# Attention scores of a head pair: products on 64 array rows per head instead of stacked high and low parts

## The chip, the cores and the metric

The kernel runs on one core of one Trainium2 chip. The metric is the device time of one execution in microseconds, the median of several runs. In the profile the engines are PE (TensorE, the matrix products; PEld its weight loads), DVE (VectorE), ACT (ScalarE), POOL (GpSimd) and SP (the queue that issues all DMAs here).

## The reference

One inference step of a two-layer decoder for a prompt of 512 tokens and 8 samples of one token each, width 1024, all in float32. Layer 0 has a gated convolution (A) and a dilated sliding-window attention (B), layer 1 a pooling mixer (C) and a retention (D). The change touches the prompt part of mixer B alone: 16 heads of 64 features; three patterns of window and dilation with ALiBi, each with its own softmax, and the three merged by their denominators.

```
for w, d in DIL_PATTERNS:            # (128,1), (512,4), (2048,16)
    ...
    s = jnp.einsum('bnirhd,bnjrhd->bnrhij', qs, kk)
    ...
    s = jnp.where(valid[None, :, None, None], s + bias, -jnp.inf)
    m = jnp.max(s, axis=-1, keepdims=True)
    p = jnp.exp(s - m)
    l = jnp.sum(p, axis=-1)
    o = jnp.einsum('bnrhij,bnjrhd->bnirhd', p, vv) / ...
...
return combine_patterns(outs, lses)
```

Merged by denominators, the three softmaxes are one softmax over all causal positions with the bias -slope x distance + log(number of patterns that hold the position); that bias is a constant array of the kernel.

## The kernel before

**Products in parts.** Each float32 operand is cut in a high part, which TensorE multiplies exactly (type fp32r), and a low part, the remainder. A large product is the sum of high x high, high x low and low x high.

**Tiles.** The input projection is worked off in tiles of 128 output features and all 520 tokens (512 of the prompt, 8 samples). A tile has 8 steps over the 1024 input features; a step (`mm3`) has six products into a tile `mm`: three parts, each in a half of 256 and a half of 264 columns. `advance` prepares the weights of later tiles at set steps: ACT writes the high half (whi), DVE the low half in two pieces (wlo).

**Order.** The order of every engine is the order in which the Python code calls it. Between two steps `tick` takes pieces of smaller work from four lists: `at(n, ...)` runs a piece n ticks later without fail, `put(..., after=n)` queues it so that one is taken per tick, ordered by its due tick, `put_fill` takes one when no `put` is due, and `put2` one every second tick. Each engine works through its own instructions strictly in that order and waits where an operand or a buffer is not ready. Small results go into a ring of four PSUM tiles `aux`, each 128 x 512.

**A head pair.** `head_pair(p)` works on two heads, 128 features, in four tiles: v, k, gate, q, so 32 ticks. What follows from the q tile of a pair therefore runs between the steps of the next pair's tiles. The pieces, with e for the head (0 or 1) and qb for a block of 128 queries:

- `k_dup`, right after the k tile: four DMAs that write each head's 64 rows of k (tile kf) to both halves of a tile kd of 128 rows. `k_split(e)`, 7 and 9 ticks after the k tile: ACT writes the high part of kd, two ticks later DVE the low part.
- After the q tile ACT writes the high part of q to the rows of the head and, a tick later, `q_lo` (DVE) the low part to the other 64 rows, scaled by -1/8. So a product of 128 rows adds high and low part of q in one go.
- `score(e, qb)`: two products, with the high and with the low part of kd, into one aux tile, over the first N = max(256, 128 (qb + 1)) keys. Then a row on DVE (L521) adds the bias and takes the minimum (the sign is turned), the next tick ACT takes the exponent with its sum ls, and two ticks later `norm` divides by the sum, on ACT for odd qb and on DVE for even.
- `turn(e, g)`: up to four transpositions of 128 x 128 of the weights into an aux tile, grouped by block of keys; `turn(e, 0)` takes the first 128 keys of all four query blocks. ACT writes the high part of it at once, DVE the low part a tick later.
- `weigh(e, jb)`: the products with v into an aux tile that stays open over jb 0 to 3.
- Beside these: `v_out` (four transpositions of v, ACT copies them and writes their high part, DVE the low part two ticks on), `q_rows` and the window scores of the samples (`window_scores`, `window_sums`, DVE), and products of the adaLN weights (`ada_mm`, on 32 columns).

The ticks after the end of the q tile at which they come due are Q0 = 5 plus a number from a table: `score(0, .)` 0, 1, 3, 4; `score(1, .)` 6, 7, 9, 10; `turn(0, .)` 11, 13, 15; `turn(1, .)` 17, 20, 22; `weigh(0, .)` 18, 19, 21, 23; `weigh(1, .)` 25 to 28.

Of the kernel before, what the change touches and what calls it, by code (L numbers as in the profile page):

```python
# [14 lines left out]
ALU = mybir.AluOpType  # L15
# [3 lines left out]
P = 128  # L19
# [10 lines left out]

# columns of the packed constants
C_ID = 0
# [54 lines left out]
def hybrid_kernel(ctx: ExitStack, tc: tile.TileContext, a, o):  # L87
# [91 lines left out]

# [1 line left out]
    now, seqn = [0], [0]  # L181
# [34 lines left out]

# [1 line left out]
    csm = cp.tile([P, C_W], F32, name="csm")  # L218
# [21 lines left out]

# [1 line left out]
    w_in = [a["w_in_e"], a["w_in_o"]]  # L242
# [61 lines left out]
    def advance(k):  # L304
        # weights of the tiles that come next, a part at each step of this tile
        if k == 1 or (k == 5 and n_split[0] < cur[0] + 2):
            w_hi()
        if k in (3, 6):
            w_lo((0,))
        if k in (4, 7):  # L310
            w_lo((1,))
        if k in (5, 7) and n_raw[0] < n_split[0] + 4:
            w_raw()
# [15 lines left out]

# [1 line left out]
    def ada_load(layer, kind, j):  # L331
# [35 lines left out]

# [1 line left out]
    def h_hi(layer, j, xp, xs):  # L369
# [12 lines left out]

# [1 line left out]
    warm = cp.tile([P, 1], F32, name="warm")  # L384
# [62 lines left out]
    load(csm[:, P:C_W], a["c_small"][:, P:C_W])  # L447
# [1 line left out]
    yB, yA = [None] * KT, [None] * KT  # L449
# [7 lines left out]
    def head_pair(p):  # L457
# [14 lines left out]

        def k_dup(kf):
            st["kd"] = []
            for e in range(2):
                kd = tt(S)
                for h in range(2):
                    load(kd[64 * h:64 * h + 64], kf[64 * e:64 * e + 64])
                st["kd"].append(kd)

        def k_split(e):
            kh, kl = tr(S), tr(S)
            act(kh, st["kd"][e])
            at(2, lo_of, kl, st["kd"][e], kh)
            st["k", e] = (kh, kl)

# [20 lines left out]

        def score(e, qb):
            if qb == 0:
                st["bt"] = bt[e]  # L510
                st["mn", e], st["ls", e] = mk(cp, [P, 4], F32, "mn", 4), mk(cp, [P, 4], F32, "ls", 4)
                st["E", e] = []
            n, N = (qb + 1) * P, max(H0, (qb + 1) * P)
            kh, kl = st["k", e]
            mn, ls = st["mn", e][:, qb:qb + 1], st["ls", e][:, qb:qb + 1]
            s = aux([P, S])
            qs = st["q", e][:, qb * P:(qb + 1) * P]
            mm(s[:, 0:N], qs, kh[:, 0:N], True, False)
            mm(s[:, 0:N], qs, kl[:, 0:N], False, True)
            sb = tt(n)  # L520
            nc.vector.tensor_tensor_reduce(  # L521
                out=sb, in0=s[:, 0:n], in1=bt[e][:, S - n:S], scale=1.0, scalar=3e38, op0=ALU.add, op1=ALU.min,
                accum_out=mn,
            )
            st["E", e].append(sb)
            at(1, act, sb, sb, ACTF.Exp, mn, -1.0, ls)
            at(3, norm, e, qb)
# [49 lines left out]

        # v, k, q and gate tiles, each followed by what depends on it
        vps = ps01[0] if p == 0 else z_tile(0, 48 + p, h0)
# [7 lines left out]
        sample_z(0, 40 + p, kps)  # L587
        at(0, k_dup, kf)
        at(1, load, o["k_t"][p], kf)
        at(7, k_split, 0)  # L590
        at(9, k_split, 1)
        gps = z_tile(0, 56 + p, h0)
# [7 lines left out]
        qps = z_tile(0, 32 + p, h0)  # L600
        for e in range(2):
            r = slice(64 * e, 64 * e + 64)
            st["q", e] = tr(S)
            act(p2(st["q", e][r]), qps[r, :, 0:H0], ACTF.Copy, scale=-0.125)

        def q_lo():
            for e in range(2):
                r, r_ = slice(64 * e, 64 * e + 64), slice(64 - 64 * e, 128 - 64 * e)
                stt(p2(st["q", e][r_]), qps[r, :, 0:H0], -0.125, p2(f(st["q", e][r])), ALU.mult, ALU.subtract)
            sample_z(0, 32 + p, qps)  # L610

        at(1, q_lo)
        for e, fn, ticks in (
            (0, score, (0, 1, 3, 4)), (1, score, (6, 7, 9, 10)), (0, turn, (11, 13, 15)), (0, weigh, (18, 19, 21, 23)),
            (1, turn, (17, 20, 22)), (1, weigh, (25, 26, 27, 28)),
        ):
            for i, n in enumerate(ticks):
                put(fn, e, i, after=Q0 + n)
# [8 lines left out]

# [1 line left out]
    uc = mk(cp, [P, KT, 15 + NB], F32, "uc", 1)[:, :, 0:2 + 2 * NB]  # L629
# [9 lines left out]
    def soft_scores():  # L639
        # softmax over window rows and the new row, (batch, head) on partitions  # L640
        prod = tt(P).rearrange("p (b k e) -> p b k e", b=NB, k=KT)
        nc.gpsimd.memset(prod, 0.0)
        for e in range(2):
            r = slice(64 * e, 64 * e + 64)
            vtt(prod[r, :, :, e].rearrange("p b k -> p k b"), zs[0][r, 32:40, :], zs[0][r, 40:48, :], ALU.mult)
        st = aux([P, 257])
        for t in range(2):
            nc.tensor.transpose(st[:, t * P:(t + 1) * P], scores[:, t].rearrange("p b h -> p (b h)"), ident)
        mm(st[:, 256:257], prod.rearrange("p b k e -> p (b k e)"), on_d[:, 0:1], True, True)
        bd = csm[:, C_BD:C_BD + 257]  # L650
        sc = tt(257)
        stt(sc[:, 0:256], st[:, 0:256], 0.125, bd[:, 0:256], ALU.mult, ALU.add)
        stt(sc[:, 256:257], st[:, 256:257], 128.0, bd[:, 256:257], ALU.mult, ALU.add)
        sm = mk(cp, [P, 2], F32, "sm", 1)
        nc.vector.tensor_reduce(out=sm[:, 0:1], in_=sc, op=ALU.max, axis=AX.X, negate=True)
        act(sc, sc, ACTF.Exp, bias=sm[:, 0:1], accum_out=sm[:, 1:2])
        nc.vector.reciprocal(sm[:, 1:2], sm[:, 1:2])
        vts(sc, sc, sm[:, 1:2], None, ALU.mult)
        soft["sc"] = sc
        put(soft_turn, after=4)  # L660
# [27 lines left out]
    def window_weigh(b0):  # L688
        # two batches at a time: rows (batch, half of the heads, head), columns (head in the half, feature)
        pd = aux([P, 512])  # L690
# [106 lines left out]

# [1 line left out]
    def out_tile(layer, m, ps, halves=(0, 1)):  # L799
# [15 lines left out]
    def scaled(j, out=None):  # L815
        # input of layer 1 without its norm's factor and without the shift
        x = xT[j] if out is None else out
        vtt(x[:, S:T], xT[j][:, S:T], mA[1][:, j, 0:NB], ALU.mult)
        act(x[:, 0:S], xT[j][:, 0:S], ACTF.Copy, scale=mA[1][:, j, 8:9])
        xT[j] = x  # L820
# [39 lines left out]

    # the first tiles of layer 1 take x without the norm's factor, which is put to their products
    h1, r1 = [[tr(), tr()] for _ in range(KT)], tt()
# [35 lines left out]

# [1 line left out]
    G = [1.0 - 2.0 ** (-5.0 - h) for h in range(H_D)]  # L900
# [6 lines left out]
    def ret_head(h):  # L907
# [97 lines left out]

        # sample group: state update and read, all batches of this head
        def v_rows():
# [64 lines left out]

        # tiles
        st["vh"] = t4(dt=F32R).rearrange("p (a i d) -> p a i d", a=4, i=2)
# [64 lines left out]

# [1 line left out]
    spl = t4()[:, 0:KT * NB * 15].rearrange("p (k b w) -> p k b w", k=KT, b=NB)  # L1141
# [76 lines left out]

# [1 line left out]
    xo = [[tt(512) for _ in range(2)] for _ in range(4)]  # L1220
# [14 lines left out]
    def rows(m, blocks):  # L1235
        # rows of tokens: their squares and their product with the gain
        hf, c = m // 4, (m % 4) * P
# [37 lines left out]

    # the last tile: one half of the tokens after the other
    m = KT - 1
# [25 lines left out]
def layout(i):  # L1303
    # the arrays in the order in which the tiles are read
    def tiles(w):
# [33 lines left out]
def results(r):  # L1339
    # features back to the last axis  # L1340
    conv = r["conv_t"].transpose(2, 1, 0).reshape(2 + 2 * NB, D)
# [29 lines left out]
```

## Time and profile before

| | |
|---|---|
| median of 3 runs | 1098.83 us (1097.79 to 1099.45) |
| span of the profiled execution | 1099.1 us; its own time is not given apart, the span lies within the runs |
| mean granted TensorE clock | 0.985 of full speed |
| layer 0, branch B (attention) | about 50 to 390 us of the span |
| PE busy | 1046.0 us, 95% |
| DVE busy | 652.6 us, 59% |
| ACT busy | 501.5 us, 46% |
| DMA | 173.15 MB, mean 158 GB/s |

L160 is the line of the helper through which every product goes, L140 that of every ACT instruction, L146 and L149 those of DVE; L543 are the transpositions of `turn`, L463 those of `v_out`, L521 the bias row of a score. So lines tell little and tiles tell more: `mm<-t,whi` is a large product, `aux<-t,t` a score product, `aux<-t,v` one of `weigh`, `aux<-big,scT` one of adaLN. All working tiles of 128 x 512 are called t. A row of the time line has the start, the length and, in brackets, the idle time ahead of it and what ended it; rows of equal form that follow each other are merged (x2, x4), and the two halves of a large product count as one form there. The length of a product contains the filling and draining of the array, so the pitch is read from start to start. A row of windows has its bounds and width, then busy time and number of instructions for PE, PEld, DVE, ACT and POOL, the granted clock, the DMA share and GB/s.

### The profile page before, as it was taken

The page shows a single profiled execution, that of the slowest core. Times are in us where ns is not written, and L with a number is a line of the kernel's source. Part 1 is how long each engine was busy: PE and PEld are TensorE (multiplying, and loading weights), DVE is VectorE, ACT ScalarE, POOL GpSimd, SP SyncE. Part 2 cuts the span into 40 slices and gives each one's busy share as a digit, 9 for nine tenths or more (in the row PEclk, how much of TensorE's full clock was granted, in tenths as well). Part 3 has the DMA queues.
Part 4 walks back from the last instruction along what each step waited for, and adds up shares of the span by engine and source line. Part 5 has one row for each costly group of instructions (what it writes and reads, how often), then busy time and mean ns, then how long its engine had stood idle before and what let it go on. Part 6 is the DMA issues. An engine that isn't in the chain of part 4 may idle for free.

```text
span 1099.1 us, 21017 instructions
## 1 busy us (share of the span) xinstructions
PE 1046.0 (95%) x8592; PEld 1000.6 (91%) x8592; DVE 652.6 (59%) x1484; ACT 501.5 (46%) x906; POOL 27.4 (2%) x45
## 2 busy tenths in 40 slices
PE   3999899989989999999999989999999999999996
PEld 1698898889989899999999989999999999999996
DVE  6557676767668544446444487555746667664443
ACT  4575568556755322223243364545444444332333
POOL 3000000000000000000000040000000000000000
PEclk9899999999999999999999999999999999999998
DMA  8365654565446463542653326372543532225212
GB/s 350 149 218 182 201 179 147 166 213 184 140 158 192 154 205 125 192 157 83 205 204 130 120 69 235 112 249 87 206 164 117 195 124 87 87 87 184 97 68 78
DMA packets 84736, 173.15 MB, mean 158 GB/s; under 512 B 7720, under 2 KB 47752, under 8 KB 81560
## 3 DMA queue, kind: packets, MB, share of 16 engines
q1 hardware_dynamic: 84640, 171.81, 46.7%
q8 instruction: 67, 1.10, 0.4%
q14 instruction: 29, 0.24, 0.1%
HBM read 149.40 MB, written 18.65 MB: 153 GB/s over the span
## 4 chain that ended last, share of the span: by engine, by line
PE 77%; DMA 8%; DVE 6%; ACT 5%; issue 2%; SPq 1%; DVEq 0%; ACTq 0%
PE mm L160 64%; PE aux L160 11%; ACT t L140 4%; DMA t<-t 4%; DMA big<-in_cache_win_k 3%; DVE t L146 2%; DVE wlo L146 1%; SPq L157 1%; DVE t L521 1%; DMA wraw<-in_w_in_e 1%; DMA v<-vdr 1%; ACT whi L140 1%; DMA out_k_t<-t 1%; ACT L140 0%; PE aux L1242 0%
## 5 line engine op out<-in xcount | busy, mean ns | idle before, releaser
L160 PE MATMUL mm<-t,whi 128*128 128x256 f32 (+1 forms) x4608 | 766.0, 288 | 7.7 <-ACT t L140 5.6
L160 PEld LDWEIGHTS mm<-t,whi 128*128 128x128 f32 x4608 | 644.3, 190 | 31.6 <-issue 17.2
L160 PE MATMUL mm<-t,wlo 128*128 128x256 f32 (+2 forms) x2304 | 468.2, 284 | 0.0
L160 PEld LDWEIGHTS mm<-t,wlo 128*128 128x128 f32 x2304 | 361.2, 190 | 0.0
L146 DVE TENSOR_TENSOR wlo<-wraw,whi 128x512 fp32r<-128x512 f32 x288 | 194.3, 701 | 51.8 <-ACT whi L140 51.3
L140 ACT ACTIVATE whi<-wraw 128x1024 fp32r<-128x1024 f32 x144 | 151.8, 1054 | 96.9 <-PE mm L160 61.1
L140 ACT ACTIVATE t<-t 128x520 fp32r<-128x520 f32 (+3 forms) x124 | 75.8, 616 | 214.8 <-DVE t L149 98.3
L146 DVE TENSOR_TENSOR t<-t,t 128x520 fp32r<-128x520 f32 (+6 forms) x172 | 112.4, 654 | 96.4 <-ACT t L140 95.0
L140 ACT ACTIVATE t<-mm 128x512 f32<-128x512 f32 (+3 forms) x124 | 61.0, 512 | 126.6 <-PE mm L160 125.9
L140 ACT ACTIVATE t<-aux 128x512 fp32r<-128x512 f32 (+7 forms) x148 | 66.5, 465 | 57.7 <-PE aux L160 20.4
L146 DVE TENSOR_TENSOR t<-aux,t 128x512 fp32r<-128x512 f32 (+6 forms) x120 | 61.7, 514 | 24.0 <-ACT t L140 17.5
L160 PE MATMUL aux<-t,v 128*128 128x512 f32 (+2 forms) x224 | 52.3, 338 | 18.5 <-DVE t L146 18.5
L160 PE MATMUL aux<-t,t 128*128 128x256 f32 (+2 forms) x320 | 63.2, 311 | 0.0
L160 PEld LDWEIGHTS aux<-t,v 128*128 128x128 f32 x224 | 36.1, 197 | 21.5 <-DVE t L146 20.4
L143 DVE COPY zs<-mm 128x8 f32<-128x8 f32 x76 | 12.2, 161 | 60.6 <-ACT t L140 60.5
L160 PEld LDWEIGHTS aux<-t,t 128*128 128x128 f32 x320 | 47.0, 188 | 0.7
L140 ACT ACT_TABLE_LOAD x32 | 41.1, 1283 | 8.1 <-DVE mn L521 3.5
L140 ACT ACTIVATE t<-t,mn 128x128 f32<-128x128 f32 (+1 forms) x64 | 35.3, 551 | 12.9 <-DVE mn L521 12.8
L521 DVE CUSTOM_DVE_ANT_0 t<-aux,t 128x128 f32<-128x128 f32 (+1 forms) x64 | 30.7, 488 | 9.6 <-PE aux L160 9.4
L149 DVE SCALAR_TENSOR_TENSOR big<-v,ksc,big 128x256 f32<-128x256 f32 x64 | 27.7, 481 | 10.1 <-ACT big L140 9.7
L146 DVE TENSOR_TENSOR t<-mm,t 128x512 f32<-128x512 f32 (+1 forms) x24 | 16.6, 690 | 26.7 <-PE mm L160 17.4
L160 PE MATMUL aux<-big,scT 128*32 128x256 f32 x384 | 27.4, 406 | 0.3 <-DMA big<-in_ada_e 0.3
(145 smaller groups left out, 591.6 us busy)
## 6 DMA issues: line engine op xcount, KB each, us to landing
wraw<-in_w_in_e SPq DMA_DIRECT2D x64, 512.0 KB
wraw<-in_w_in_o SPq DMA_DIRECT2D x48, 512.0 KB
big<-in_ada_e SPq DMA_DIRECT2D x12, 1024.0 KB
big<-in_ada_o SPq DMA_DIRECT2D x12, 1024.0 KB
wraw<-in_w_out_e SPq DMA_DIRECT2D x16, 512.0 KB
big<-in_state_ret SPq DMA_DIRECT2D x16, 512.0 KB
out_new_ret_sample<-big SPq DMA_DIRECT2D x16, 512.0 KB
wraw<-in_w_out_o SPq DMA_DIRECT2D x16, 512.0 KB
```

The costliest lines, as they stand in the source:

```text
L140: return nc.scalar.activation(out=out, in_=in_, func=func, scale=scale, **kw)
L143: return nc.vector.tensor_copy(out, in_)
L146: return nc.vector.tensor_tensor(out=out, in0=in0, in1=in1, op=op)
L149: return nc.vector.scalar_tensor_tensor(out=out, in0=in0, scalar=scalar, in1=in1, op0=op0, op1=op1)
L157: return nc.sync.dma_start(out=out, in_=in_)
L160: nc.tensor.matmul(out, lhsT=lhsT, rhs=rhs, start=start, stop=stop)
L521: nc.vector.tensor_tensor_reduce(out=sb, in0=s[:, 0:n], in1=bt[e][:, S - n:S], scale=1.0, scalar=3e38, op0=ALU.add, op1=ALU.min, accum_out=mn,
```

## The change

The copy of k goes (`k_dup`); `k_split` runs once for both heads, 3 ticks after the k tile, on kf itself. The high part of q is one tile of 128 rows for both heads, the low part another. `score(qb)` does both heads at once: three products for each, high x high, high x low (of k) and low x high, each on the 64 rows of its head, rows 0 to 63 for head 0 and 64 to 127 for head 1, the two heads alternating and each into an aux tile of its own. The term low x low, which the stacked form contained, is left out. `soft(e, qb, s)` is the rest of the old `score`.

The table changes too: `score` 0, 2, 4, 7 after Q0; `turn(0, .)` 9, 11, 14; `turn(1, .)` 12, 15, 18; `weigh(0, .)` 17, 19, 20, 21; `weigh(1, .)` 22, 23, 25, 26. `norm` of block 3 still comes three ticks after its score, at Q0 + 10, and `turn(0, 0)` now stands at Q0 + 9: it takes the first 128 keys of block 3 of head 0 before they are divided by their sum.

```diff
-        def k_dup(kf):
-            st["kd"] = []
-            for e in range(2):
-                kd = tt(S)
-                for h in range(2):
-                    load(kd[64 * h:64 * h + 64], kf[64 * e:64 * e + 64])
-                st["kd"].append(kd)
-
-        def k_split(e):
+        def k_split(kf):
             kh, kl = tr(S), tr(S)
-            act(kh, st["kd"][e])
-            at(2, lo_of, kl, st["kd"][e], kh)
-            st["k", e] = (kh, kl)
+            act(kh, kf)
+            at(2, lo_of, kl, kf, kh)
+            st["k"] = (kh, kl)
...
-        def score(e, qb):
+        def score(qb):
+
+            N = max(H0, (qb + 1) * P)
+            ss_ = [aux([P, S]) for _ in range(2)]
+            for c, (x, y) in enumerate(((0, 0), (0, 1), (1, 0))):
+                for e in range(2):
+                    r = slice(64 * e, 64 * e + 64)
+                    mm(ss_[e][:, 0:N], st["q"][x][r, qb * P:(qb + 1) * P], st["k"][y][r, 0:N], c == 0, c == 2)
+            for e in range(2):
+                soft(e, qb, ss_[e])
+
+        def soft(e, qb, s):
             if qb == 0:
-                st["bt"] = bt[e]
                 st["mn", e], st["ls", e] = mk(cp, [P, 4], F32, "mn", 4), mk(cp, [P, 4], F32, "ls", 4)
                 st["E", e] = []
-            n, N = (qb + 1) * P, max(H0, (qb + 1) * P)
-            kh, kl = st["k", e]
+            n = (qb + 1) * P
             mn, ls = st["mn", e][:, qb:qb + 1], st["ls", e][:, qb:qb + 1]
-            s = aux([P, S])
-            qs = st["q", e][:, qb * P:(qb + 1) * P]
-            mm(s[:, 0:N], qs, kh[:, 0:N], True, False)
-            mm(s[:, 0:N], qs, kl[:, 0:N], False, True)
...
-        at(0, k_dup, kf)
         at(1, load, o["k_t"][p], kf)
-        at(7, k_split, 0)
-        at(9, k_split, 1)
+        at(3, k_split, kf)
...
-        for e in range(2):
-            r = slice(64 * e, 64 * e + 64)
-            st["q", e] = tr(S)
-            act(p2(st["q", e][r]), qps[r, :, 0:H0], ACTF.Copy, scale=-0.125)
+        qh, ql = tr(S), tr(S)
+        st["q"] = (qh, ql)
+        act(p2(qh), qps[:, :, 0:H0], ACTF.Copy, scale=-0.125)
 
         def q_lo():
-            for e in range(2):
-                r, r_ = slice(64 * e, 64 * e + 64), slice(64 - 64 * e, 128 - 64 * e)
-                stt(p2(st["q", e][r_]), qps[r, :, 0:H0], -0.125, p2(f(st["q", e][r])), ALU.mult, ALU.subtract)
+            stt(p2(ql), qps[:, :, 0:H0], -0.125, p2(f(qh)), ALU.mult, ALU.subtract)
             sample_z(0, 32 + p, qps)
 
         at(1, q_lo)
+        for qb, n in enumerate((0, 2, 4, 7)):
+            put(score, qb, after=Q0 + n)
         for e, fn, ticks in (
-            (0, score, (0, 1, 3, 4)), (1, score, (6, 7, 9, 10)), (0, turn, (11, 13, 15)), (0, weigh, (18, 19, 21, 23)),
-            (1, turn, (17, 20, 22)), (1, weigh, (25, 26, 27, 28)),
+            (0, turn, (9, 11, 14)), (1, turn, (12, 15, 18)), (0, weigh, (17, 19, 20, 21)), (1, weigh, (22, 23, 25, 26)),
         ):
```

What this makes of the order is shown at three places, all in the fifth pair.

On PE, the score products of the query block qb = 2, before for head 0 (aux_470, followed by block 3, aux_474) and, further on, head 1 (aux_493); the first name is what is written, then the keys, then the queries:

```order
L160 MATMUL aux_470_2562<-t_433_2344,t_456_2471 128x384
L160 MATMUL aux_470_2562<-t_434_2345,t_456_2471 128x384
...
L160 MATMUL aux_474_2580<-t_433_2344,t_456_2471 128x512
L160 MATMUL aux_474_2580<-t_434_2345,t_456_2471 128x512
...
L160 MATMUL aux_493_2666<-t_440_2374,t_457_2473 128x384
L160 MATMUL aux_493_2666<-t_441_2375,t_457_2473 128x384
```

and after the change, one block for both heads:

```order
L160 MATMUL aux_460_2569<-t_410_2283,t_438_2456 128x384
L160 MATMUL aux_461_2570<-t_410_2283,t_438_2456 128x384
L160 MATMUL aux_460_2569<-t_411_2284,t_438_2456 128x384
L160 MATMUL aux_461_2570<-t_411_2284,t_438_2456 128x384
L160 MATMUL aux_460_2569<-t_410_2283,t_439_2457 128x384
L160 MATMUL aux_461_2570<-t_410_2283,t_439_2457 128x384
```

Four products of two heads, in two places, became six in one place.

On ACT, the part of the next pair's k in the gate tile. Before (t_502 and t_503 are the copies kd, aux_513 and aux_525 the turns (1,0) and (1,1) of the pair ahead):

```order
228 L140 ACTIVATE t_514_2784<-aux_513_2779 128x512
229 L140 ACTIVATE t_516_2794<-t_502_2711 128x512
230 L140 ACT_TABLE_LOAD
231 L140 ACTIVATE t_519_2810<-mm_501_2704 128x512
232 L140 ACTIVATE t_523_2824<-t_503_2714 128x512
233 L140 ACTIVATE t_526_2832<-aux_525_2828 128x384
```

and after (t_483 is kf, which ACT writes from mm_459; aux_485, aux_491 and aux_495 are the turns (1,0), (0,2) and (1,1)):

```order
215 L140 ACTIVATE t_483_2693<-mm_459_2561 128x512
216 L140 ACTIVATE t_486_2710<-aux_485_2705 128x512
217 L140 ACTIVATE whi_488_2719<-wraw_421_2339 128x1024
218 L140 ACTIVATE t_489_2729<-t_483_2693 128x512
219 L140 ACTIVATE t_492_2738<-aux_491_2733 128x512
```

The high part of k waited for a DMA's tile ahead of the turns' evacuations; now it reads a tile that ACT wrote itself three instructions before.

On ACT again, from the normalisation of block 1 to the first turn. Before, for head 1 (aux_497 is `turn(0,0)`, of the other head):

```order
219 L140 ACTIVATE t_485_2628<-t_485_2628,ls_480_2608 128x256
220 L140 ACTIVATE t_494_2669,ls_480_2608<-t_494_2669,mn_479_2607 128x384
221 L140 ACTIVATE t_496_2684,ls_480_2608<-t_496_2684,mn_479_2607 128x512
222 L140 ACTIVATE t_498_2698<-aux_497_2693 128x512
223 L140 ACTIVATE t_500_2701<-mm_473_2570 128x512
```

and after, for both heads (t_474 is block 3 of head 0, aux_477 is `turn(0,0)`, which reads it):

```order
203 L140 ACTIVATE t_454_2538<-t_454_2538,ls_446_2507 128x256
204 L140 ACTIVATE t_455_2540<-t_455_2540,ls_449_2511 128x256
205 L140 ACTIVATE t_462_2577,ls_446_2507<-t_462_2577,mn_445_2506 128x384
206 L140 ACTIVATE t_463_2579,ls_449_2511<-t_463_2579,mn_448_2510 128x384
207 L140 ACTIVATE t_466_2600<-aux_465_2595 128x512
208 L140 ACTIVATE v_467_2602<-t_466_2600 128x8x64
209 L140 ACTIVATE t_474_2640,ls_446_2507<-t_474_2640,mn_445_2506 128x512
210 L140 ACTIVATE t_475_2642,ls_449_2511<-t_475_2642,mn_448_2510 128x512
211 L140 ACTIVATE t_478_2666<-aux_477_2661 128x512
212 L140 ACTIVATE t_474_2640<-t_474_2640,ls_446_2507 128x512
```

The exponents and normalisations of the two heads, which stood in different stretches, stand next to each other, and the evacuation of the first turn follows directly on the exponents of block 3.

## The prediction

> **What bounds the kernel now.** I read the page first: how much of the span the TensorE works, and which engine the chain of work that ended last runs over.
>
> ```profile
> span 1099.1 us, 21017 instructions
> PE 1046.0 (95%) x8592; PEld 1000.6 (91%) x8592; DVE 652.6 (59%) x1484; ACT 501.5 (46%) x906; POOL 27.4 (2%) x45
> PE 77%; DMA 8%; DVE 6%; ACT 5%; issue 2%; SPq 1%; DVEq 0%; ACTq 0%
> ```
>
> PE is the bound: busy for 95%, and 77% of the chain. The other engines matter only where PE waits for them. Then I read the waits of the attention stage alone (55 to 390 us), columns: us in total, times, longest.
>
> ```profile
> ACT t L140 <- DMA t<-t: 47.7, 7, 8.0
> PE aux L160 <- DVE t L146: 19.0, 9, 3.5
> DVE big L146 <- DMA big<-in_cache_win_k: 7.6, 7, 1.8
> ```
>
> PE idles 19.0 us, always in front of a product into aux with the VectorE named. But the longest waits on another engine are ScalarE's, 47.7 us for a DMA from t to t, and `k_dup` issues the only such copies. The time line of one pair, ScalarE, VectorE and PE, shows that the two are one event.
>
> ```profile
> 120.51 0.60 ACT L140 ACTIVATE t<-aux 128x512 fp32r<-128x512 f32 x1 [1.00 <-PE aux L543]
> 129.11 0.63 ACT L140 ACTIVATE t<-t 128x512 fp32r<-128x512 f32 x1 [8.00 <-DMA t<-t]
> 132.07 0.48 ACT L140 ACTIVATE t<-aux 128x384 fp32r<-128x384 f32 x1
> ...
> 132.58 0.56 DVE L146 TENSOR_TENSOR t<-aux,t 128x384 fp32r<-128x384 f32 x1
> ...
> 133.19 1.04 PE L160 MATMUL aux<-t,v 128*128 128x512 f32 x2 [3.55 <-DVE t L146]
> ```
>
> ScalarE, which works in order, stands 8.00 us in `k_split(0)` until the copy of k has landed. Behind it waits the evacuation of `turn(1,1)` (132.07); its low half follows on VectorE (132.58, done at 133.14), and only then is an accumulator of the ring of four free for `weigh(1,0)`, which starts at 133.19. Such a wait comes once a pair. A second cost follows it, which the granted clock shows (the column before the DMA share):
>
> ```profile
> 100.00:150.00 50.00, 46.45 (x369) 44.81 (x368) 35.30 (x94) 32.34 (x66) 0.00 (x0) 0.97 0.47 148
> 200.00:250.00 50.00, 44.32 (x342) 42.09 (x342) 32.34 (x76) 32.71 (x59) 0.00 (x0) 0.93 0.51 161
> 300.00:350.00 50.00, 46.26 (x369) 43.65 (x368) 38.05 (x86) 27.75 (x53) 0.50 (x4) 0.97 0.56 173
> ```
>
> In these three windows the clock fell for a while behind a long wait. The loss is 50 x (0.03 + 0.07 + 0.03) = 6.5 us, in four falls. The border lies between these two waits, the first without a fall behind it, the second with one:
>
> ```profile
> 96.72 0.73 PE L160 MATMUL aux<-t,v 128*128 128x512 f32 x2 [2.15 <-DVE t L146]
> ...
> 204.47 0.73 PE L160 MATMUL aux<-t,v 128*128 128x512 f32 x2 [2.46 <-DVE t L146]
> ```
>
> **The change, part by part.** *The copy of k goes.* Four DMAs a pair vanish, and `k_split` reads a tile that ScalarE wrote three steps earlier, so nothing holds ScalarE there: -19.0 us of PE idling and -6.5 us of slow clock. I take the whole of both; the lower bound of this gain is in the rivals.
>
> *Less work beside PE.* Per pair ScalarE loses one 512-wide split (0.63, the row at 129.11) and one of two query rows, VectorE one low half of k and one of q. Both engines have room (59% and 46%), so nothing is booked for it; if the room were gone, these would be a gain of the same kind, so it costs nothing either way.
>
> *The score products.* Two rows of now, and what stands next on PE, give the pitch:
>
> ```profile
> 105.99 0.52 PE L160 MATMUL aux<-t,t 128*128 128x384 f32 x2
> 106.34 0.64 PE L160 MATMUL mm<-t,whi 128*128 128x256 f32 x4
> 106.82 0.40 PE L160 MATMUL mm<-t,wlo 128*128 128x256 f32 x2
> 107.06 0.62 PE L160 MATMUL aux<-t,t 128*128 128x512 f32 x2
> 107.52 0.64 PE L160 MATMUL mm<-t,whi 128*128 128x256 f32 x4
> ```
>
> Two products take 0.24 us at 256 columns (106.82 to 107.06, a large product's, of one form with the scores'), 0.35 at 384, 0.46 at 512; a head has four blocks, 256, 256, 384 and 512 wide: 1.29 us. Sixteen heads: 20.6 us. After the change a pair has three products per block and head, of 64 rows each, the heads alternating. If the two heads' products run side by side on their halves of the array, a block costs three pitches for both heads: 1.5 x 1.29 = 1.94 us a pair, 15.5 us in all. One after the other they cost 31.0. No row here has 64 rows; the nearest are the adaLN products on 32 columns, four of which belong to different column groups:
>
> ```profile
> 127.33 0.39 PE L160 MATMUL mm<-t,wlo 128*128 128x256 f32 x2
> 127.65 1.07 PE L160 MATMUL aux<-big,scT 128*32 128x256 f32 x16
> 128.65 0.75 PE L160 MATMUL mm<-t,whi 128*128 128x256 f32 x4
> 129.24 0.40 PE L160 MATMUL mm<-t,wlo 128*128 128x256 f32 x2
> ...
> L160 PE MATMUL aux<-big,scT 128*32 128x256 f32 x384 | 27.4, 406 | 0.3 <-DMA big<-in_ada_e 0.3
> ```
>
> Sixteen of 0.41 us, 6.5 us of product, stand within 1.07 us: sixfold overlap, where four full products (0.28 each, 1.1 us) in 0.64 overlap less than twofold. So parts of the array do work side by side, and I take 15.5, with 31.0 as the other bound.
>
> The same rows price the change of shape: 0.32 instead of 0.24 ahead of the sixteen, 0.59 instead of 0.48 for the four behind them, so 0.19 for both ways, and a drain inside the 1.00 us that I can't separate, so up to 0.3. Against it, a transposition to 8 columns costs nothing beyond its own length:
>
> ```profile
> 108.00 0.40 PE L160 MATMUL mm<-t,wlo 128*128 128x256 f32 x2
> 108.23 0.27 PE L489 MATMUL aux<-csm,zs 128*8 128x128 f32 x1
> 108.26 0.72 PE L160 MATMUL mm<-t,whi 128*128 128x256 f32 x4
> 108.82 0.41 PE L160 MATMUL mm<-t,wlo 128*128 128x256 f32 x2
> ```
>
> From 108.00 to 108.82 is 0.82: 0.24 for two, 0.48 for four, 0.10 for it. There are 32 blocks, so 0 to 9.6 us; I take 0.15 each, 4.8, the middle between the two rows, as both are of columns and neither of rows. Score products in sum: 15.5 + 4.8 - 20.6 = -0.3 us.
>
> The Trainium skill, TensorEngine Tiling (Array Packing), section Key Properties, says that changing the tiling mode drains the TensorE. By it each block pays the drain twice, and with the 0.3 of the adaLN rows the time would be 4.8 us over mine; without any drain 4.8 under it. The adaLN rows agree with the rule, the transposition does not show it.
>
> *A new wait at the first turn.* The order moves too: block 3 of both heads stands at step 12 and `turn(0,0)`, whose fourth transposition reads block 3's exponents, at step 14. Before, seven steps lay between a head's block 3 and its first turn. What lies on the way I price by the rows in which ScalarE and VectorE do the same work now:
>
> ```profile
> 112.02 0.58 ACT L140 ACTIVATE t<-aux 128x512 f32<-128x512 f32 x1
> 112.63 0.64 ACT L140 ACTIVATE v<-t 128x512 fp32r<-128x512 f32 x1
> 113.34 0.51 ACT L140 ACTIVATE t<-t,ls 128x256 f32<-128x256 f32 x1
> 113.76 0.60 ACT L140 ACTIVATE t<-t,mn 128x384 f32<-128x384 f32 x1
> 114.63 0.72 ACT L140 ACTIVATE t<-t,mn 128x512 f32<-128x512 f32 x1 [0.18 <-DVE mn L521]
> ...
> 112.66 0.56 DVE L521 CUSTOM_DVE_ANT_0 t<-aux,t 128x384 f32<-128x384 f32 x1 [0.52 <-PE aux L160]
> 113.15 0.16 DVE L531 RECIPROCAL ls<-ls 128x1 f32<-128x1 f32 x1
> 113.30 0.69 DVE L146 TENSOR_TENSOR v<-t,v 128x512 fp32r<-128x512 f32 x1
> 113.91 0.68 DVE L521 CUSTOM_DVE_ANT_0 t<-aux,t 128x512 f32<-128x512 f32 x1
> ```
>
> I count from the end of block 2's products. VectorE: two 384-wide bias rows (0.49 from start to start) and the reciprocal of block 1: 1.13. ScalarE: two normalisations of block 1 (0.42 each), two exponents of block 2 (0.60 each), the copy and the high half of v (0.61 + 0.64): to 4.42. VectorE: low half of v, which needs that high half, 0.61, then block 3's bias row, 0.68: to 5.71. ScalarE: exponent of block 3, 0.72: 6.43. PE needs for the same stretch five steps of 0.72 (106.34 to 107.06), 3.60; v's four transpositions at the 0.10 of the one at 108.23, 0.40; block 3's products 0.69 + 0.15; three transpositions of the turn 0.30: 5.14. The turn thus waits 6.43 - 5.14 = 1.3 us, 10 us in eight pairs, below the 2.15 us that left the clock alone. Bounds: 0, if ScalarE and VectorE run ahead, and 2.2. Behind this wait stand the large products of the next tile; two steps on, `turn(0,1)` needs the normalisation of the same block, which may add a few tenths.
>
> The sum: -19.0 - 6.5 - 0.3 + 10.4 = -15.4. The profiled execution has a span of 1099.1 us; its own time is not given apart, and the three timed runs have a median of 1098.8, so the span can be taken as the time. Forecast: 1084 us.
>
> **The rivals.** *No new wait.* ScalarE and VectorE keep up, for ScalarE sheds work: 1099.1 - 25.5 - 0.3 = 1073; without a cost of the shape 1068.5. Against it: in the rows above ScalarE has no gap over 0.2 us from 112.02 to 114.63 as it is.
>
> *The halves do not run side by side.* 31.0 + 4.8 - 20.6 = +15.2; the turn, reached later, waits perhaps 0.7 (5.6 in all): 1099.1 - 25.5 + 15.2 + 5.6 = 1094; with 0.3 a block 1099. Only the columns' rows speak against it.
>
> The Trainium skill, TensorE: Matmul & The Clock Gate, Part 3, says that products on different row groups start about 4 ns apart and run concurrently, and gives 3.07 times for four of 32 rows. By it 15.5 stands and this rival falls; no run so far shows row groups.
>
> *Slower: the turn's wait passes the clock's border.* If the chain to block 3's exponent is 1.1 us longer than I count (ScalarE still behind from the steps before), the wait is 2.4 us; the clock then falls as it did behind 2.46, for 6.5/4 = 1.6 us more. Eight times 4.0 is 32: 1099.1 - 25.5 - 0.3 + 32 = 1105. It decides from about 2.3 us on; my 1.3 speaks against it, that the chain runs over two busy engines for it.
>
> *The copy was not the cause.* VectorE also waits for the cached keys (7.6 us in total); if half of PE's idling hangs on that, 9.5 and some 3 of clock stay, with the new wait: about 1096. The row [8.00 <-DMA t<-t] speaks against it.
>
> **How the numbers follow.** Forecast 0.50; no new wait 0.20; halves in turn 0.15; slower 0.08; copy not the cause 0.07. The forecast's own range, by 4.8 of shape and 6 of the turn, is 1074 to 1095. For 8 in 10 the range reaches to the no-wait case without cost of shape and to the upper end of the halves in turn: 1068 to 1100. A difference under 0.2% (2.2 us) can't be told from none here. Faster than 1096.6: all but a little of the first, the second, two thirds of the third, half of the last: 0.80; same 0.08; slower 0.12.
>
> **What would show it.** No wait of ScalarE on t<-t and no PE idling of 2 to 3.5 us at `weigh(1,0)`; the clock at 1.00 in the windows from 50 to 350. Products of the form 64*128, in pairs that start together (three pitches a block) or one by one (six). A PE idle of about 1.3 us at the fourth transposition of `turn(0,0)`, released by ScalarE's exponent; none shows the 1073 right, one over 2.3 with a clock below 1.00 the 1105. The prediction is wrong if the pairs start one by one, or if a wait of another kind (cached keys, accumulators) takes up the gain.

## The result, and the profile after

The changed kernel takes 1132.8 us (median of 4 runs, 1130.21 to 1135.08); the kernel before, on the same chip, 1098.67. The ratio is 1.0302, with a 95% interval of 1.0272 to 1.0333: slower by 3%, where I had forecast 1084 and a range of 1068 to 1100. The profiled execution took 1130.21 us itself, its span is 1128.4: 29.3 us over the span of before.

The page of the changed kernel (span; PE's share; the chain that ended last):

```profile
span 1128.4 us, 21065 instructions
PE 1055.3 (94%) x8656; PEld 996.1 (88%) x8656; DVE 643.7 (57%) x1468; ACT 490.2 (43%) x890; POOL 27.4 (2%) x45
PE 82%; DMA 8%; DVE 4%; ACT 4%; issue 1%; SPq 0%; DVEq 0%; ACTq 0%
PE mm L160 67%; PE aux L160 13%; DMA big<-in_ada_o 7%; ACT t L140 3%; DVE t L146 1%; DVE t L518 1%; DVE wlo L146 1%; DMA v<-vdr 1%; PE aux L540 1%; ACT v L140 0%; PE aux L348 0%; DVE v L146 0%; DMA t<-in_x_t 0%; PE aux L1235 0%; SPq L157 0%
```

Work beside PE fell as the change says (DVE from 652.6 to 643.7, ACT from 501.5 to 490.2), and the chain now holds a load that nobody spoke of: 7% of it is `big<-in_ada_o`, the adaLN weights of layer 1. The waits of the attention stage (55 to 390 us; us in total, times, longest) show where PE stands:

```profile
PE aux L160 <- DMA big<-in_ada_o: 30.4, 8, 5.0
PE aux L540 <- ACT t L140: 8.0, 8, 1.1
PE aux L160 <- DVE t L146: 0.5, 1, 0.5
```

The 19.0 us in front of `weigh` are gone (0.5 is left), and no wait of ScalarE on the copy exists any more. So that step held. The wait at the first turn is there, 8.0 us. But 30.4 us are new: once in each of eight pairs PE waits up to 5.0 us for the adaLN weights. The granted clock (the column before the DMA share) follows:

```profile
50.00:100.00 50.00, 44.23 (x353) 40.54 (x352) 26.51 (x63) 28.26 (x51) 0.00 (x0) 0.97 0.53 179
100.00:150.00 50.00, 44.68 (x356) 41.22 (x354) 30.08 (x71) 25.81 (x49) 0.00 (x0) 0.97 0.40 127
150.00:200.00 50.00, 44.70 (x365) 40.43 (x361) 31.86 (x90) 29.79 (x65) 0.00 (x0) 1.00 0.44 141
200.00:250.00 50.00, 41.77 (x333) 38.17 (x331) 29.13 (x67) 27.57 (x55) 0.00 (x0) 0.97 0.55 159
250.00:300.00 50.00, 43.38 (x336) 39.21 (x337) 29.85 (x68) 24.96 (x48) 0.00 (x0) 0.93 0.47 156
300.00:350.00 50.00, 43.90 (x347) 40.45 (x347) 29.22 (x70) 25.96 (x49) 0.10 (x1) 0.93 0.41 127
```

The loss is 50 x (0.03 + 0.03 + 0.03 + 0.07 + 0.07) = 11.5 us, where before it was 6.5. The window from 150 to 200 has no fall, though one of the eight waits lies in it:

```profile
171.67 1.07 PE L160 MATMUL aux<-big,scT 128*32 128x256 f32 x16 [3.12 <-DMA big<-in_ada_o]
```

So the border that the prediction drew between waits of 2.15 and 2.46 us is no rule of length alone: 3.12 us left the clock at 1.00 here. What decides it besides the length, no run shows.

**One such wait.** The time line of PE (first two rows) and of the DMA queue SP with ScalarE's copy of v (after that), same pair:

```profile
127.47 0.39 PE L160 MATMUL mm<-t,wlo 128*128 128x256 f32 x2
132.09 1.72 PE L160 MATMUL aux<-big,scT 128*32 128x256 f32 x16 [4.23 <-DMA big<-in_ada_o]
...
117.44 0.57 ACT L140 ACTIVATE t<-aux 128x512 f32<-128x512 f32 x1
...
118.04 0.39 SPq L157 DMA_DIRECT2D out_new_win_v_prompt<-t  x1
118.94 0.31 SPq L157 DMA_DIRECT2D v<-qdr  x1
119.32 2.10 SPq L157 DMA_DIRECT2D big<-in_cache_win_k  x3
121.52 1.95 SPq L157 DMA_DIRECT2D big<-in_ada_o  x1
```

The same queue in the kernel before:

```profile
111.95 0.68 SPq L157 DMA_DIRECT2D v<-qdr  x1
112.73 4.21 SPq L157 DMA_DIRECT2D big<-in_cache_win_k  x3
116.99 1.69 SPq L157 DMA_DIRECT2D big<-in_ada_o  x1
118.77 0.41 SPq L157 DMA_DIRECT2D out_new_win_v_prompt<-t  x1
```

Two things moved that neither the diff's lines nor my sum name. First, the store of v stood behind the load of the adaLN weights and now stands ahead of it, with four transfers between them. In these rows SP issues in the order of the program, and this store is issued at 118.04, as ScalarE's copy of v ends (117.44 + 0.57): the loads behind it wait for ScalarE. The weights are issued at 121.52 instead of 116.99. Second, the products with these weights, `ada_mm`, are a `put_fill` piece that takes the first tick that no `put` claims. In the kernel before, the table of scores, turns and weighs left no tick for it until 15 ticks after the load in the program's order. The new table has four pieces fewer (four scores instead of eight) and leaves a tick free 9 ticks after the load. The store moved for the same reason: `v_out` is a `put_fill` piece too and comes three ticks earlier, the loads only two. The issue takes 1.95 us, the weights land 8.2 us after that (the time from DMA to landing that the trace has for this tile), so at 131.7; the products start at 132.09, and PE had been free for them since 127.9 (4.23 earlier). For the kernel before, the same reckoning gives 116.99 + 1.69 + 8.2 = 126.9, an estimate, and the products started at 127.65: 0.8 us of cover.

### The profile page after: what moved, and what is told of

Read it like the earlier page. It is cut to its first block, busy times and chain, and to the rows that moved or that the text cites. A ratio compares the mean times of both kernels' runs of the same rounds, so it can differ in the third digit from the quotient of the medians.

```text
span 1128.4 us, 21065 instructions
## 1 busy us (share of the span) xinstructions
PE 1055.3 (94%) x8656; PEld 996.1 (88%) x8656; DVE 643.7 (57%) x1468; ACT 490.2 (43%) x890; POOL 27.4 (2%) x45
## 3 DMA queue, kind: packets, MB, share of 16 engines
q8 instruction: 68, 1.11, 0.4%
## 4 chain that ended last, share of the span: by engine, by line
PE 82%; DMA 8%; DVE 4%; ACT 4%; issue 1%; SPq 0%; DVEq 0%; ACTq 0%
PE mm L160 67%; PE aux L160 13%; DMA big<-in_ada_o 7%; ACT t L140 3%; DVE t L146 1%; DVE t L518 1%; DVE wlo L146 1%; DMA v<-vdr 1%; PE aux L540 1%; ACT v L140 0%; PE aux L348 0%; DVE v L146 0%; DMA t<-in_x_t 0%; PE aux L1235 0%; SPq L157 0%
## 5 line engine op out<-in xcount | busy, mean ns | idle before, releaser
L146 DVE TENSOR_TENSOR t<-t,t 128x520 fp32r<-128x520 f32 (+6 forms) x164 | 107.0, 652 | 96.3 <-ACT t L140 94.6
L140 ACT ACTIVATE t<-t 128x520 fp32r<-128x520 f32 (+3 forms) x116 | 70.9, 616 | 166.8 <-DVE t L149 98.1
L140 ACT ACTIVATE t<-mm 128x512 f32<-128x512 f32 (+2 forms) x116 | 56.2, 506 | 114.0 <-PE mm L160 112.5
L160 PE MATMUL aux<-big,scT 128*32 128x256 f32 x384 | 31.5, 454 | 31.1 <-DMA big<-in_ada_o 30.4
L160 PE MATMUL aux<-t,t 64*128 64x256 f32 (+6 forms) x384 | 56.1, 329 | 0.0
L140 ACT ACTIVATE t<-t,mn 128x128 f32<-128x128 f32 (+3 forms) x64 | 35.4, 553 | 35.3 <-DVE mn L518 35.3
L160 PEld LDWEIGHTS aux<-big,scT 128*32 128x32 f32 x384 | 12.0, 122 | 41.1 <-DVE t L146 26.0
L160 PEld LDWEIGHTS aux<-t,t 64*128 64x128 f32 (+1 forms) x384 | 41.5, 186 | 5.4
L140 ACT ACTIVATE md<-aux 128x256 f32<-128x256 f32 x24 | 9.2, 382 | 82.8 <-PE aux L160 82.8
L518 DVE CUSTOM_DVE_ANT_0 t<-aux,t 128x128 f32<-128x128 f32 (+3 forms) x64 | 28.8, 488 | 21.0 <-PE aux L160 20.3
```

The lines of the kernel that those rows point to most:

```text
L140: return nc.scalar.activation(out=out, in_=in_, func=func, scale=scale, **kw)
L146: return nc.vector.tensor_tensor(out=out, in0=in0, in1=in1, op=op)
L160: nc.tensor.matmul(out, lhsT=lhsT, rhs=rhs, start=start, stop=stop)
L518: nc.vector.tensor_tensor_reduce(out=sb, in0=s[:, 0:n], in1=bt[e][:, S - n:S], scale=1.0, scalar=3e38, op0=ALU.add, op1=ALU.min, accum_out=mn,
```

## The experiments

All edits are of the changed kernel, except in the last two runs. Ratios are against the kernel before, run beside them. The changed kernel, and with it all variants but e4, e5, e9 and e10, takes the first keys of block 3 of head 0 into the turn before they are divided by their sum, so it leaves out that division for them; that moves no work of PE.

**Which of the two moves costs the 30 us (e1, e2, e3).** e1 puts the adaLN pieces eight ticks later, e2 the store of v three ticks later, behind the loads, e3 both.

```diff
-            at(8, ada, 1, "ss", p, raw)
+            at(16, ada, 1, "ss", p, raw)        # e1, e3
-            at(1, load, wv[:, :, p * P:(p + 1) * P], p4(vtm))
+            at(4, load, wv[:, :, p * P:(p + 1) * P], p4(vtm))   # e2, e3
```

> The changed kernel with one number altered: the adaLN weights' products of a pair are queued 16 ticks after the load of those weights, not 8, so that they stand at tick 29 after the q tile, as before the change, and not at tick 21. Theory A (the looser table of the change lets these products slip forward to a place where their weights have not landed; that is the whole loss): the PE wait on big<-in_ada_o (30.4 us) and the clock's falls behind it (23.9 us at half, 11.9 us lost) go, about 1086 to 1090 us, no other PE wait over 2 us. Theory B (the DMA queue of SP is held up by the store of v, which waits for ScalarE's copy, so that keys and adaLN weights come 3 to 4 us late): the keys are still late, VectorE still waits for them, and PE, no longer stopped at the adaLN products, now waits at the turn (1,2) for the accumulator that VectorE frees, about 1.8 us a pair: 1100 us. Theory C (the adaLN products only show a delay that another engine would cause anyway): 1115 us or more.

> The changed kernel with one number altered: the store of v goes out 4 ticks after its copy was issued, not 1, so that in the DMA queue it stands behind the loads of the window's keys and of the adaLN weights, as before the change. The adaLN products stay at tick 21. Theory A: the weights still have too little time (8.2 us of landing and 2 us of issue against some 11 us), so a wait of 3 us or more a pair stays, with the clock's falls: 1110 to 1120 us. Theory B: the issue comes about 3.3 us earlier, the wait shrinks from 4.4 to about 1.1 us a pair and the clock no longer falls: about 1090 us. Theory C: 1115 us or more.

> Both of these alterations together. Theories A and B alike: about 1086 us, with only the wait of 1.4 us a pair at the first turn left and no fall of the clock between 50 and 350 us; if it is no faster than the better of the two single ones, the other alteration is idle. Theory C: no better than 1110 us.

| run | median us | ratio (95%) | span | PE waits for in_ada_o |
|---|---|---|---|---|
| e1 | 1088.6 | 0.9918 (0.9903 to 0.9932) | 1086.7 | none |
| e2 | 1093.62 | 0.9959 (0.9936 to 0.9982) | 1091.5 | 3.9 us |
| e3 | 1090.27 | 0.993 (0.9915 to 0.9945) | 1088.5 | none |

To undo either is enough, or nearly: the wait needs both, the earlier products and the later load (with the earlier products alone, in e2, 3.9 us of it stay). e3 is no faster than e1 but 1.7 us slower, with ranges that do not meet; its second edit adds nothing there, and I can't place the 1.7. In e2 the weights are issued at 114.11 for 2.22 us, and the products that wait for them start at 124.35; the reckoning above, issue plus 8.2, gives 124.5. e1 is 41.7 us of span under the changed kernel, and the two rows of the profile, 30.4 of waiting and 11.5 of clock, make 41.9. With the weights in time the products take what they took before, and the clock is 1.00 in all windows from 50 to 350 (time line of e1):

```profile
129.16 0.39 PE L160 MATMUL mm<-t,wlo 128*128 128x256 f32 x2
129.49 1.07 PE L160 MATMUL aux<-big,scT 128*32 128x256 f32 x16
130.49 0.75 PE L160 MATMUL mm<-t,whi 128*128 128x256 f32 x4
```

So the accident is explained. But the repaired change gains 9 us, not 15.

**The wait at the first turn (e4, e5).** Both are e3 with another table: e4 has that of the kernel before, e5 that table with head 0's first turn two ticks later still, behind the normalisation.

```diff
-            (0, turn, (9, 11, 14)), (1, turn, (12, 15, 18)), (0, weigh, (17, 19, 20, 21)), (1, weigh, (22, 23, 25, 26)),
+            (0, turn, (13, 14, 16)), (0, weigh, (18, 19, 21, 23)), (1, turn, (17, 20, 22)), (1, weigh, (25, 26, 27, 28)),   # e5
```

> Both alterations, and the table of before for turns and weighing (first turn at tick 16 instead of 14, behind the normalisation of block 3, so that every block is transposed normalised). The prediction's term for the first turn (1.3 us a pair, measured at 1.36) goes: 11 us under e3_both, about 1075 us. If the time only moves to the next place where PE needs ScalarE or VectorE (weighing at ticks 23 to 33, two ticks later than in e3_both), no more than 3 us are gained.

> e3_both with a table in which turn(0,0) stands at tick 18 after the q tile (14 in the change, 16 in e4_both_old_turns), the other turns of head 0 at 19 and 21, and head 1's turns and all weighing as before the change; every block is transposed normalised. In e4 the fourth transposition of the first turn still waited 1.24 us a pair. Theory 1 (that wait is the time that the chain of both heads' exponents and normalisations needs, and two more ticks, 1.5 us of PE work, cover it): the wait is gone, 8 x 1.2 = 10 us under e3, about 1080 us. Theory 2 (PE only waits elsewhere instead, at the weighing that follows closer on its turn): within 3 us of e3, 1087 to 1091 us.

e4: 1089.08 us, 0.9921 (0.9904 to 0.9937). e5: 1090.5 us, 0.9923 (0.9904 to 0.9942). Neither differs from e3. Both divide every block by its sum before it is turned, so the repaired change costs no more with that division in its place. In e4 the turn still waits, for the normalisation now (7.1 us); in e5 it doesn't, but PE waits for the low halves of the turns at `weigh` instead (waits of e5, 55 to 390 us):

```profile
PEld aux L160 <- DVE t L146: 9.7, 9, 1.9
PE aux L160 <- DVE t L146: 8.3, 10, 1.7
```

8.3 us there, 7.8 at the turn in e3. Moving the piece moves the wait. The likely reason is that the chain over VectorE and ScalarE from block 3's scores to the last weigh stays as long as it is, and that with both heads' scores in one piece head 0's block 3 comes at tick 7 instead of 4; no run tests this apart.

**The change of shape (e6).** e3 with blocks 0 and 1 of both heads in one piece: 24 changes of shape instead of 32.

```diff
-        for qb, n in enumerate((0, 2, 4, 7)):
-            put(score, qb, after=Q0 + n)
+        for qbs, n in (((0, 1), 1), ((2,), 4), ((3,), 7)):
+            put(score, *qbs, after=Q0 + n)
```

> e3_both with the scores of query blocks 0 and 1 in one piece at tick 6, both in one accumulator tile per head, so that the array changes its shape 24 times forth and back instead of 32. If each change costs the 0.28 us that the trace of the changed kernel shows around a block (0.09 ahead, 0.10 inside, 0.09 behind), it gains 8 x 0.28 = 2.3 us: 1088.0 us. If the cost of a block lies elsewhere (in the semaphores or the first weight load of a block, whatever its shape), the second block of the piece shows the same cost and nothing is gained: 1090.3 us.

1092.14 us, 0.9935 (0.992 to 0.9951): no gain in the total, which lies above both expected values. What became of it the time lines show, first one block of the changed kernel, then the merged piece of e6:

```profile
187.24 0.40 PE L160 MATMUL mm<-t,wlo 128*128 128x256 f32 x2
187.57 0.62 PE L160 MATMUL aux<-t,t 64*128 64x256 f32 x6
188.12 0.75 PE L160 MATMUL mm<-t,whi 128*128 128x256 f32 x4
188.71 0.40 PE L160 MATMUL mm<-t,wlo 128*128 128x256 f32 x2
```

```profile
174.12 0.40 PE L160 MATMUL mm<-t,wlo 128*128 128x256 f32 x2
174.44 0.98 PE L160 MATMUL aux<-t,t 64*128 64x256 f32 x12
175.35 0.74 PE L160 MATMUL mm<-t,whi 128*128 128x256 f32 x4
175.93 0.28 PE L160 MATMUL mm<-t,wlo 128*128 128x256 f32 x1
```

Two large products and four take 0.24 and 0.48, three pitches of 256 columns 0.36: 1.08. The block needs 188.71 - 187.24 = 1.47, so one change of shape there and back costs 0.39. In e6 the piece holds six pitches, 1.44 in all, and needs 1.81: 0.37 for both blocks together. Eight changes of 0.39 less are 3 us; but the wait at the first turn grew from 7.8 to 12.3 us (in this piece four bias rows and four exponents come due at once; whether that is why, no run shows). By the time lines the gain was there, and the next wait took it up.

**Whether the two heads have to alternate (e7).** e3 with the two loops the other way round, so that all three products of head 0 come ahead of those of head 1:

```diff
-            for c, (x, y) in enumerate(((0, 0), (0, 1), (1, 0))):
-                for e in range(2):
+            for e in range(2):
+                for c, (x, y) in enumerate(((0, 0), (0, 1), (1, 0))):
```

> e3_both with the three products of head 0 ahead of the three of head 1 instead of alternating. If products of the two halves of the array run side by side only where they are neighbours in the order, a block now has five pitches instead of three (only the third of head 0 and the first of head 1 overlap): 2 x 0.645 us a pair more, 10.3 us in all, of which the wait at the first turn hides some: 1096 to 1100 us. If TensorE takes products ahead out of order, nothing changes: 1090 us.

1089.82 us, 0.9912 (0.9896 to 0.9929): no loss at all, the second of the two expected values. The time line of e7:

```profile
170.79 0.40 PE L160 MATMUL mm<-t,wlo 128*128 128x256 f32 x2
171.12 0.62 PE L160 MATMUL aux<-t,t 64*128 64x256 f32 x6
171.67 0.75 PE L160 MATMUL mm<-t,whi 128*128 128x256 f32 x4
172.25 0.40 PE L160 MATMUL mm<-t,wlo 128*128 128x256 f32 x2
```

172.25 - 170.79 = 1.46, as with alternating heads; six products one by one would need 0.36 more. The single starts are in the last section.

**What the copy of k costs (e8, e9, e10).** e8 is e3 with the four DMAs back and the split of each head 7 and 9 ticks after the k tile. e9 and e10 are the kernel before, copy and stacked products as they were, with two numbers changed:

```diff
-        at(7, k_split, 0)
-        at(9, k_split, 1)
+        at(15, k_split, 0)    # e10: 11
+        at(17, k_split, 1)    # e10: 13
```

> e3_both with the four copies of k by DMA back as before the change, and k split per head from them 7 and 9 ticks after the k tile (32 of the products' operands thus come from the copy; their values are the same). Theory 1 (the prediction's: ScalarE stands in the split until the copy has landed, PE waits for what is queued behind, and the clock falls): ScalarE waits 5 to 8 us a pair for t<-t, PE 2 to 3.5 us, 19.0 + 6.5 us in all as before the change: 1110 to 1116 us. Theory 2 (in the new order ScalarE has slack at this place): less than 5 us, up to 1095 us.

> The kernel before with its copy of k and its stacked products, and one edit: the two splits of k stand 15 and 17 steps after the k tile instead of 7 and 9, still ahead of the first score (21). The copy takes as long as ever, but ScalarE comes to it about eight steps of 0.8 to 0.9 us later, so its wait of 6 to 8 us a pair (47.7 in all) should be a few tenths, and what stands behind it in ScalarE's order, the evacuations of the second head's turns, is no longer held. Theory 1 (TensorE's idling of 19.0 us and the clock's falls worth 6.5 come from the place of the split in the order, not from the copy as such): both vanish, 1099 - 25.5 = 1073 to 1078, below every kernel with the change, since neither the change of shape (+4) nor the wait at the first turn (+10) is there. Theory 2 (the accumulators are short for another reason, the copy's wait only names the last releaser): idling stays near 10 to 19 us and the time at 1090 to 1099.

> The same with the splits 11 and 13 steps after the k tile, four steps later than before, some 3.5 us. Theory 1: ScalarE's wait goes from 6 to 8 us to 2.5 to 4.5 us a pair, and the turns' evacuations of the pair before, which stand within the next few steps, get out ahead of it for the most part: TensorE's idling under 5 us and no fall of the clock, 1073 to 1082. Theory 2: as the kernel before less a third at most, 1090 to 1099.

| run | median us | ratio (95%) | span | ScalarE waits for the copy |
|---|---|---|---|---|
| e8 | 1090.41 | 0.9921 (0.9901 to 0.9941) | 1088.9 | 23.0 us |
| e9 | 1075.6 | 0.9778 (0.9748 to 0.9808) | 1072.3 | 0.4 us |
| e10 | 1074.82 | 0.977 (0.9741 to 0.9798) | 1075.2 | 21.6 us |

e9 and e10 are 24 us faster than the kernel before and the fastest of all, with the copy in them. The waits of e10, 55 to 390 us:

```profile
ACT t L140 <- DMA t<-t: 21.6, 7, 4.8
DVE big L146 <- DMA big<-in_cache_win_k: 10.3, 9, 2.8
PE aux L160 <- DVE t L146: 3.2, 4, 1.2
PE aux L160 <- DMA big<-in_ada_o: 1.4, 2, 1.1
```

In e8 and e10 ScalarE still waits 23.0 and 21.6 us for the copy, and PE idles 0.5 and 3.2 us at `weigh`, not 19.0. ScalarE in e9, over the second head's turns of the pair that the prediction's first time line shows:

```profile
116.94 0.60 ACT L140 ACTIVATE t<-aux 128x512 fp32r<-128x512 f32 x1 [0.58 <-PE aux L543]
...
120.23 0.49 ACT L140 ACTIVATE t<-aux 128x384 fp32r<-128x384 f32 x1 [0.78 <-PE aux L543]
...
126.47 0.63 ACT L140 ACTIVATE t<-t 128x512 fp32r<-128x512 f32 x1
```

The evacuation of `turn(1,1)` runs at 120.23 and no longer behind the split (before: 129.11 and then 132.07); the split comes at 126.47 and waits for nothing. So the copy cost time only because the split that waits for it stood in ScalarE's order ahead of evacuations that PE needed. Between the 1075 to 1076 of e10 and e9 and the 1089 to 1090 of the repaired change lie 13 to 15 us. The score products (+7.3, below) and the wait at the first turn (8.0) make 15.3; against them stand the 2.8 and 3.2 us that PE still waits at `weigh` in e9 and e10, where the repaired change has 0.5. That leaves some 13; the rest I can't place.

## Why the prediction was wrong, step by step

- **The copy of k goes, -19.0 and -6.5: right in size, by its mechanism too.** PE's wait at `weigh` fell to 0.5 us; e9, which takes ScalarE's wait away and nothing else, measured -24 in the median and -27 in the span. What the step didn't ask is whether the copy has to go for it. It hadn't: two numbers do the same, and e8, the new order with the copy back, loses nothing.
- **The score products, -0.3: mis-sized.** The halves do run side by side: three pitches a block, 15.5 us as booked. The term of the shape was 0.15 a block, 4.8 us, with 0.3 as upper bound; it is 0.39, so 12.5 us. The products cost 15.48 + 12.48 - 20.64 = +7.3. I had taken the middle between the adaLN rows and a transposition; the adaLN rows were the nearer of the two, and on the 64-row visits the part inside, which I had called inseparable, is as large as the 0.19 that I saw outside. The Trainium skill, TensorEngine Tiling (Array Packing), Key Properties, says that a change of the tiling mode drains the TensorE. The trace agrees as far as each change costs time, 0.39 us there and back; that this is a drain it doesn't show, and the page gives no size.
- **The new wait at the first turn, +10.4: the mechanism right, the size partly by luck.** The rows of the changed kernel at the place that the prediction counted, ScalarE and then PE:

```profile
196.72 0.63 ACT L140 ACTIVATE v<-t 128x512 fp32r<-128x512 f32 x1
198.72 0.72 ACT L140 ACTIVATE t<-t,mn 128x512 f32<-128x512 f32 x1 [1.37 <-DVE mn L518]
...
192.78 0.74 PE L160 MATMUL mm<-t,whi 128*128 128x256 f32 x4
...
197.99 0.49 PE L540 MATMUL aux<-csm,t 128*128 128x128 f32 x3
199.59 0.33 PE L540 MATMUL aux<-csm,t 128*128 128x128 f32 x1 [1.11 <-ACT t L140]
```

The fourth transposition would have begun 0.32 after 197.99 and begins at 199.59: 1.28 us late against 1.3. Of it 1.11 is idle time in the profile, 8.0 in eight pairs, the last of which has less. In the place of the gap of at most 0.2 that ScalarE had before, it now waits 1.37 for the bias row. The difference came out better than its two sums: from 192.78, where block 2's products are done, PE needs 5.53 us to that transposition where I counted 5.14, and the chain over VectorE and ScalarE 6.81 where I counted 6.43. Both are 0.4 short, and the two misses cancel.

- **"The sum": the step that failed.** It has no term for what the table moves beside the pieces it lists. The order was compared at scores, turns and splits; `ada_mm`, `v_out`'s store and SP's queue were left out, though the queue of every moved piece is part of the order. The row that would have warned stands in the prediction itself, quoted for another purpose: `aux<-big,scT` at 127.65, whose weights were issued at 116.99 and landed, by the reckoning above, 0.8 us ahead of use. That missing term is 30.4 us, and 11.5 of clock behind it.
- **The account.** -18.5 - 6.5 + 7.3 + 8.0 + 30.4 + 11.5 = +32.2 against 29.3 of span (18.5 because 0.5 of the 19.0 is left). The 2.9 between them I can't place; e9 and e10, equal in the median, differ by 2.9 in the span.
- **The rivals.** "Slower: the turn's wait passes the clock's border" had the right sign and the wrong place: the turn stayed at 1.3 and the clock fell behind another wait; its border at about 2.3 us did not hold as a rule, as the wait of 3.12 above shows. "No new wait" fell at the first turn. "The halves do not run side by side" and "the copy was not the cause" fell. The last sentence of the prediction, on a wait of another kind that takes up the gain, is what came; it had no price and, in effect, no chance.

## What to carry to other kernels

When a table of due times is loosened, list every piece that fills its gaps and every transfer in the queues between, and work out for each the time from its load's issue to its use: a filler with 0.8 us of cover slides forward as soon as a tick is free. Before removing a transfer on which an engine waits, ask what stands behind the waiting instruction; moving that instruction behind it (two numbers, -2.2%) was worth more here than removing the transfer and changing the products to suit (-0.8% after repair). Pieces of another array shape pay the change per visit, here 0.39 us, so they want to be few and long; e6 showed that in its time line, not in its total.

## What the runs showed of the hardware that I had not expected

A visit of products on 64 rows between products on 128 costs 0.39 us, in four parts of about 0.1 each: ahead of the first product, between the first pair and the second, ahead of the first large product and between it and the next (in e3's visit at 172.18 us these are 0.21, 0.22, 0.20 and 0.22 from start to start, where the pitch is 0.12). It is 0.39 at 256, 384 and 512 columns alike. The last two of the four are easily missed, since they stand behind the visit.

The products of the two heads start side by side even where the program has all three of head 0 ahead of those of head 1. Starts in us of the six products of a block of 256 columns, from the trace, alternating (e3) and one head after the other (e7):

```
e3  172.177 172.180   172.398 172.402   172.512 172.515
e7  171.117 171.127   171.339 171.349   171.454 171.464
```

That each pair is one product of each head, and the program's fourth product starts ahead of its second, can be read from the semaphore operations that the packed trace keeps with each record. In this block of e7's program the first product (head 0) waits for ScalarE, the second signals, the third waits for VectorE, and the fourth, head 1's first, waits for a signal of PE itself. In the trace the same four stand at the first, the third, the fifth and the second start, and so they do in the first block of seven of the eight pairs. So what stands ahead of the prediction, that each engine works strictly in its own order, is not so for the starts of these products.

The Trainium skill, TensorE: Matmul & The Clock Gate, Part 3, has products start in strict program order and says that different row groups start about 4 ns apart; the 3 to 4 ns of e3 agree with it. The order of e7's starts, fourth ahead of second, differs from it, and there the measurement decides.
